# Loading x in column quarters ahead of the weights each multiplies, in a two-layer encoder trunk on one core

## The chip, the cores and the metric

The kernel runs on one core of one Trainium2 chip. The metric is the device time of one execution in microseconds. The engines are named as in the profile: PE is TensorE (PEld its weight loads), ACT is ScalarE, DVE is VectorE, POOL is GpSimd, SP is SyncE; SPq and ACTq are the parts of SP and ACT that issue DMA transfers.

## What is computed

x has 256 rows of 1024 columns. Two layers follow one another; layer 0 mixes tokens with a recurrence (RWKV-7), layer 1 with stick-breaking attention:

```python
def swiglu(x, w_gate, w_up, w_down):
    return (jax.nn.silu(x @ w_gate) * (x @ w_up)) @ w_down

for i in range(DEPTH):
    x = layer_norm(ALPHA * x + 0.5 * swiglu(x, ffn1_w_gate[i], ffn1_w_up[i], ffn1_w_down[i]), ...)
    proj = x @ (rwkv_w_in if i == 0 else sb_w_in)
    heads = concatenate([mix(proj[...]), memory_attention(proj[...], mem_k, mem_v)])
    x = layer_norm(ALPHA * x + heads @ w_out[i], ...)
    x = layer_norm(ALPHA * x + 0.5 * swiglu(x, ffn2_w_gate[i], ffn2_w_up[i], ffn2_w_down[i]), ...)
```

All is float32, and the weights (301 MB read in all) pass through the core once.

## The kernel before, in words

The 256 rows are two halves of 128 (`hf` 0 and 1). Both lie transposed in `xTh` and `xTl`: a float32 value is split into a part that the fast matmul format float32r holds (`hi`, copied out by ACT) and the rest (`lo`, subtracted by DVE). A product of x with weights is three matmuls in one PSUM bank: hi·hi, hi·lo, lo·hi (`mm3`). The 2816 columns of a feed-forward layer are cut into 11 blocks of 256 (`ffn_block`). A block's gate and up weights come as four *pieces* of two k-rows each (`piece`: 256 KB of gate and 256 KB of up into one `raw` buffer, then `hi` by ACT and `lo` by DVE); k runs over the 8 column groups of x. The first block of the program multiplies both halves, with one PSUM bank for each.

No engine's order is that of the code. `Plan` records every operation; `order` then simulates the engines with a cost model (`LAND` is the time it gives a transfer to land) and takes operations by priority; `issue` emits them. The priorities are a table found offline by a search over the same model (`URGENCY`). Operations recorded inside `nc.together()` go out as one. Because everything is emitted at one place, nearly all instructions have line L789 in the profile (L786 in the changed kernel). DMA transfers carry eight completion semaphores in turn, so the ninth is issued only when the first has landed. SP issues nearly all transfers, in order; those of the first piece are issued by ACT.

At the start, nine matmuls on zeros (`warm`) run while data come in. `load_x(hf)` loads one half of x in two transfers of 512 columns (256 KB each) and `turn_x` transposes it in two groups of four on PE (the identity matrix for it is in `cst`), each followed by one ACT copy to `xTh` and one DVE subtraction to `xTl`. Half 0 is loaded before the first block is recorded, half 1 inside it; the plan puts half 1's transfers after all four pieces of the first block:

```python
    load_x(0)
    warm(WARM[1], max(o.i for o in nc.ops if o.eng == "PE"))
```

In the profile of before, the first piece is `raw_9r`, `hi_7r`, `lo_8r`; the next three are 12/10/11, 15/13/14 and 18/16/17 in the same sense. `ps_29r` is the bank of half 0, `ps_30r` that of half 1, `ps_5r` and `ps_6r` are the banks for transposes, `ps_3r` receives the warming matmuls.

Of the kernel before, what the change touches and what calls it, by code (L numbers as in the profile page):

```python
# [129 lines left out]
LAND = 3200.0  # L130
WINDOW = 3413.0
# [12 lines left out]
    '(T`_hY~DVEN35^W4I!+&C&ovw2;nl<9cVu{J+8+e$5`KWUv=*t_B-LL7>nq84K*52IfUm5h49A{A=GjF=juLjK#aSe)PsjZxaG+h=fc8+B|})ChI'
    '^g=n(LR_9^-x1S#e>Et$&Mg<6~-HFoe<eI(fHxFIAg6V>~c0ggdQeaVvOR8sjqSXzF^0_5a-55W0R5WA{lhe%dR9#gE1~y<d!5yTZxUA$(sxgf;f'
    'wd0vcn>rel^F^;_@gq%%6n42RNe#xnh*1Dr}2;Vtx!95{tdmx1WI>$JESO_hqy7w|YX&vLYKg5_#&r^@UuIqd~O~2m=;a#s6hMB&7V;uH-2ysG;Z'
    'y$_tPs0$_=ZkSlwNyB-H^s-s_*#h&vZrG_Qx4W=+tWuO9C|Ls8<YMO3t`vgF~)B~m^$43N5N}M$5Vr0Wpj+ZvSkUSYUBx7&i@nh)Jlam*QDe2i_&'
    'ovEH`k>Y`rO74-fLCLU;G-+23oP_xr`U&xJ6knp%$zVeNnE_)Bg5?H}XcpSzd3%&QZ^mXqmtv}`Ke3*RND$G8h-U+o&>$+q_RPzb$RhcM>l7;{@|'
    'o?7sJV~kI`?%|ng1~bjC3E>#rmbfy68LrU{mb3o>8+q|GhVWrd=c!+9SjvTm<u8gct?uXC>#plV7&R2OX2kfrTD}Fd9qNT}YLjww#OoC?F2U2+-j'
    '4AJxX$Ns^sx}Wm>T0OxOnD7I<CDk6{_mf>ccpu2XE^0@1tV8xKRi<)s68UkKe&yWt^XdJ4>dAP^xi^t6;I+@)&c#+r;hZSTL0e|JH_6xcur<IL#k'  # L150
    'I_v$eoKa>iCFHgsbFf!G3&RWR-TBKt+9C~L}jAyS-g%Llb<43ODp*?=kp2n-_nm#wEhLfG}dwU4=@MFO{A#83A2Q_fF4_%`RrDw(1;U?Vvn05?>*'
    'B@yRuI^s|XY}x#{w*CDW1ZO{e1k7XXkz*ic<CELEqgzFC>=k$&K_w(kvl@T2A)U4=Pvg@i*o}<*z;Am0ekEB!R0sUSaMwm52^K2IR4f5>A0T`tl5'
    'R%*3-Hj?c3;Dbm}$rF9~1W2FLj44863!Rdwv6W-9cckyUnwaBWS!IT6C7-_o(6wVl%Ed*G&k`qttpZ`_QNG;GyYwSK|t>htiF7-!ZEVg5(-;!zrZ'
# [1775 lines left out]
```

## Time and profile before

| | us |
|---|---|
| median of 3 runs | 1057.22 |
| lowest, highest | 1055.42, 1058.07 |
| span of the profiled execution | 1055.1 |
| PE busy | 1039.6 (99% of the span) |
| DVE busy, ACT busy | 885.9 (84%), 740.6 (70%) |

The time of the profiled execution is not listed apart from its span; the span is 0.3 us below the lowest and 2.1 us below the median of the three runs. A span runs from the first to the last instruction. PE's matmuls are pipelined, and a busy share near 100% says that the queue of matmuls is never empty, not that the array is at its peak. Rows of the timeline read: start, duration, engine, line, operation, output<-inputs, shapes, how many merged; in brackets the idle time ahead and what ended it.

### The profile page before, as it was taken

The numbers are of one execution on the slowest core, as the hardware profiler recorded it, in microseconds if no ns is written. First come the engines' busy times: TensorE is split into PE (matmuls) and PEld (weight loads), VectorE is DVE, ScalarE is ACT, GpSimd is POOL, SyncE is SP. The second block draws the span as 40 slices with busy tenths as digits, with TensorE's granted clock in tenths as the row PEclk, the third lists the DMA queues.
The fourth block names the chain that finished last, engine by engine and source line by source line (L and its number), as shares of the span: only waits on it lengthen the run. The fifth ranks groups of instructions, "written<-read, shape, count | busy, mean of one in ns | idle before, by whom it ended". The sixth has DMA issues, their size and how long they took to land.

```text
span 1055.1 us, 17845 instructions
## 1 busy us (share of the span) xinstructions
PE 1039.6 (99%) x6275; PEld 833.2 (79%) x6275; DVE 885.9 (84%) x1241; ACT 740.6 (70%) x1064; POOL 5.3 (0%) x20
## 2 busy tenths in 40 slices
PE   8999999999899999999999999999999999999997
PEld 7888888877688776788888888888778777778885
DVE  6776579999899997898799765569899999976788
ACT  6665568878789877567678454557987998765663
POOL 0000000000000000000000000000000000000000
PEclk9999999999999999999999999999999999999999
DMA  9997869879499788799999966758989989998892
GB/s 314 339 366 252 265 202 352 276 239 328 152 326 332 261 270 281 245 352 324 288 346 346 328 205 217 233 187 286 370 303 322 363 278 322 333 348 266 280 316 80
DMA packets 212684, 303.19 MB, mean 287 GB/s; under 512 B 13892, under 2 KB 159728, under 8 KB 212594
## 3 DMA queue, kind: packets, MB, share of 16 engines
q1 hardware_dynamic: 212050, 301.53, 85.8%
q8 instruction: 49, 0.80, 0.3%
q10 hardware_dynamic: 544, 0.52, 0.2%
q14 instruction: 41, 0.34, 0.1%
HBM read 300.95 MB, written 1.05 MB: 286 GB/s over the span
## 4 chain that ended last, share of the span: by engine, by line
PE 96%; DVE 1%; DMA 1%; SPq 0%; ACT 0%; issue 0%; DVEq 0%; ACTq 0%
PE ps_29r L789 29%; PE ps_30r L789 28%; PE ps_25r L789 8%; PE ps_27r L789 8%; PE ps_26r L789 8%; PE ps_3r L789 8%; PE ps_5r L789 3%; PE ps_6r L789 3%; DMA raw_9r<-in_ffn_w_down_dram 1%; DMA raw_12r<-in_ffn_w_up_dram 0%; DVE x L789 0%; SPq L789 0%; DVE L_345r L789 0%; DVE st_573r L789 0%; DVE idle_2r L789 0%
## 5 line engine op out<-in xcount | busy, mean ns | idle before, releaser
L789 PE MATMUL ps_30r<-lo_11r,xTh 128*128 128x512 f32 x78 | 30.4, 390 | 0.0
L789 PE MATMUL ps_29r<-lo_11r,xTh 128*128 128x512 f32 (+1 forms) x76 | 29.3, 386 | 0.6 <-DVE lo_11r L789 0.6
L789 ACT ACTIVATE idle_2r<-ps_29r 128x256 f32<-128x256 f32 (+1 forms) x35 | 14.8, 424 | 17.1 <-PE ps_29r L789 16.7
L789 ACT ACTIVATE idle_1r<-ps_30r 128x256 f32<-128x256 f32 (+1 forms) x31 | 12.9, 417 | 18.5 <-PE ps_30r L789 18.4
L789 PE MATMUL ps_30r<-hi_13r,xTh 128*128 128x512 f32 x60 | 24.5, 408 | 0.0
L789 PE MATMUL ps_30r<-lo_41r,xTh 128*128 128x512 f32 x62 | 24.2, 390 | 0.0
L789 PE MATMUL ps_30r<-hi_40r,xTh 128*128 128x512 f32 (+1 forms) x60 | 23.8, 396 | 0.0
L789 PE MATMUL ps_30r<-hi_13r,xTl 128*128 128x512 f32 x60 | 23.5, 391 | 0.0
L789 ACT ACTIVATE idle_2r<-ps_30r 128x256 f32<-128x256 f32 (+1 forms) x23 | 9.9, 432 | 19.2 <-PE ps_30r L789 19.2
L789 PE MATMUL ps_30r<-lo_14r,xTh 128*128 128x512 f32 x60 | 23.4, 390 | 0.0
L789 PE MATMUL ps_29r<-hi_13r,xTh 128*128 128x512 f32 (+1 forms) x56 | 23.1, 413 | 0.0
L789 PE MATMUL ps_30r<-hi_40r,xTl 128*128 128x512 f32 (+1 forms) x60 | 23.0, 384 | 0.0
L789 PE MATMUL ps_29r<-lo_17r,xTh 128*128 128x512 f32 (+1 forms) x60 | 23.0, 383 | 0.0
L789 PE MATMUL ps_29r<-hi_10r,xTh 128*128 128x512 f32 x56 | 22.8, 407 | 0.0
L789 PE MATMUL ps_29r<-lo_14r,xTh 128*128 128x512 f32 x58 | 22.6, 390 | 0.0
L789 PE MATMUL ps_29r<-hi_7r,xTh 128*128 128x512 f32 x54 | 22.3, 413 | 0.2 <-ACT xTh L789 0.2
L789 ACT ACT_TABLE_LOAD x16 | 20.5, 1283 | 2.0 <-issue 1.7
L789 PE MATMUL ps_29r<-hi_10r,xTl 128*128 128x512 f32 x56 | 21.9, 392 | 0.0
L789 PE MATMUL ps_29r<-lo_41r,xTh 128*128 128x512 f32 x56 | 21.8, 390 | 0.0
L789 PE MATMUL ps_29r<-hi_49r,xTh 128*128 128x512 f32 x54 | 21.7, 401 | 0.0
L789 PE MATMUL ps_29r<-hi_13r,xTl 128*128 128x512 f32 (+1 forms) x56 | 21.5, 383 | 0.0
L789 PE MATMUL ps_29r<-hi_7r,xTl 128*128 128x512 f32 x54 | 21.2, 393 | 0.2 <-DVE xTl L789 0.2
(2160 smaller groups left out, 3936.6 us busy)
## 6 DMA issues: line engine op xcount, KB each, us to landing
raw_9r<-in_ffn_w_down_dram SPq DMA_DIRECT2D x22, 512.0 KB, 5.8
raw_12r<-in_ffn_w_down_dram SPq DMA_DIRECT2D x19, 512.0 KB, 5.3
raw_48r<-in_ffn_w_gate_dram SPq DMA_DIRECT2D x36, 256.0 KB, 4.8
raw_48r<-in_ffn_w_up_dram SPq DMA_DIRECT2D x36, 256.0 KB, 5.3
raw_18r<-in_ffn_w_gate_dram SPq DMA_DIRECT2D x32, 256.0 KB, 4.6
raw_18r<-in_ffn_w_up_dram SPq DMA_DIRECT2D x32, 256.0 KB, 5.5
raw_51r<-in_ffn_w_gate_dram SPq DMA_DIRECT2D x31, 256.0 KB, 5.0
raw_51r<-in_ffn_w_up_dram SPq DMA_DIRECT2D x31, 256.0 KB, 5.9
```

Source lines behind the costliest of these rows:

```text
L789: fn(*[at(x) for x in a], **{n: at(x) for n, x in k.items()})
```

## The change

- x is loaded as eight transfers of 128 x 256 (128 KB): for each quarter of the columns, one of half 0 and one of half 1. In the code a quarter stands ahead of the piece of weights that it multiplies. Before there were four transfers of 128 x 512.
- The first piece comes in four transfers of 128 KB in place of two of 256 KB: those of its first k-row from ACT, those of its second from SP.
- The transposes of a quarter are recorded just ahead of the products that use it: the first quarter as two groups of two (one for each half), the others as one group of four over both halves, so that one copy and one subtraction serve both. There are 32 transposes in all before and after.
- The products of k below 4 in the first block are recorded singly and no longer three together, so the plan may put other work between them.
- The cost model takes 1700 ns and not 3200 for a transfer to land in the first 6 us, and the table of priorities is a new one. It reorders blocks of matmuls in many places of the program.

```diff
-XPARTS = 2
+LAND0 = 1700.0
+SOON = 6000.0
-URGENCY = ( ... )
+URGENCY = ( ... )
-                landed = max(t + LAND + 400.0 * o.fine, landed) + o.kb * 1024 / 330.0
+                landed = max(t + (LAND if t >= SOON else LAND0) + 400.0 * o.fine, landed) + o.kb * 1024 / 330.0
...
-        made = [(queue or nc.sync).dma_start(v(raw)[..., i * m:(i + 1) * m], src) for i, src in enumerate(srcs)]
+        if queue is None:
+            made = [nc.sync.dma_start(v(raw)[..., i * m:(i + 1) * m], src) for i, src in enumerate(srcs)]
+        else:
+            made = [(nc.sync if k else queue).dma_start(v(raw)[:, k, i * m:(i + 1) * m], src[:, k])
+                    for k in range(shape[0]) for i, src in enumerate(srcs)]
+            for o in made[2:]:
+                nc.in_turn("load", o)
...
-    def mm3(o, sh, sl, wh, wl, start, stop):
+    def mm3(o, sh, sl, wh, wl, start, stop, apart=False):
+        if apart:
+            nc.tensor.matmul(o, sh, wh, start=start, stop=False)
+            nc.tensor.matmul(o, sh, wl, start=False, stop=False)
+            nc.tensor.matmul(o, sl, wh, start=False, stop=stop)
+            return
...
-    def load_x(hf):
-        xs[hf] = xp.tile([P, D], F32, tag=f"x{hf}", name=nm("x"))
-        for n in range(XPARTS):
-            sl = slice(n * D // XPARTS, (n + 1) * D // XPARTS)
+    def load_x(g):
+        sl = slice(2 * g * P, 2 * (g + 1) * P)
+        for hf in range(NHALF):
             nc.in_turn("load", nc.sync.dma_start(xs[hf][:, sl], x[0, half_sl(hf), sl]))
-        turn_x(hf)
+    def turn_part(g):
+        for both in [range(NHALF)] if g else [[hf] for hf in range(NHALF)]:
+            pt = ps("tp")
+            n = len(both)
+            with nc.together():
+                for j in range(2):
+                    for i, hf in enumerate(both):
+                        at = slice((j * n + i) * P, (j * n + i + 1) * P)
+                        nc.tensor.transpose(pt[:, at], xs[hf][:, (2 * g + j) * P:(2 * g + j + 1) * P], ident)
+            sp = pt[:, :2 * n * P].rearrange("p (k t) -> p k t", k=2)
+            hi, lo = (t[:, 2 * g:2 * g + 2, both[0] * P:(both[-1] + 1) * P] for t in xTt)
+            nc.scalar.activation(hi, sp, AF.Copy)
+            nc.vector.tensor_sub(lo, sp, hi.bitcast(F32))
...
+        for k in range(KT):
+            if begin and k % 2 == 0:
+                turn_part(k // 2)
+                if k == 0:
+                    warm(WARM[1], max(o.i for o in nc.ops if o.eng == "PE"))
+            wh, wl = (t[:, k % 2] for t in gu[k // 2])
+            for hf in halves:
+                mm3(o[hf], xT[hf][0][:, k], xT[hf][1][:, k], wh, wl, k == 0, k == KT - 1, begin and k < 4)
...
-    load_x(0)
-    warm(WARM[1], max(o.i for o in nc.ops if o.eng == "PE"))
```

The order that the plan makes of it stands below for the three places that matter. `x_78` is half 0 and `x_79` half 1 in both kernels. In the changed kernel the first piece is `raw_8r`, `hi_6r`, `lo_7r`, the second `raw_11r`, `hi_9r`, `lo_10r`, the third `raw_14r`; `ps_28r` is the bank of half 0, `ps_29r` that of half 1, `ps_30r` and `ps_31r` are the banks for transposes.

The issue of transfers at the start on SP, before:

```order
L789 DMA cst<-in_const_dram 128x128
L789 DMA x_78<-in_x_dram 128x512 x2
L789 DMA raw_12r<-in_ffn_w_gate_dram 128x2x256
L789 DMA raw_12r<-in_ffn_w_up_dram 128x2x256
L789 DMA raw_15r<-in_ffn_w_gate_dram 128x2x256
L789 DMA raw_15r<-in_ffn_w_up_dram 128x2x256
L789 DMA raw_18r<-in_ffn_w_gate_dram 128x2x256
L789 DMA raw_18r<-in_ffn_w_up_dram 128x2x256
L789 DMA x_79<-in_x_dram 128x512 x2
```

and now:

```order
L786 DMA x_79<-in_x_dram 128x256
L786 DMA raw_8r<-in_ffn_w_gate_dram 128x256
L786 DMA raw_8r<-in_ffn_w_up_dram 128x256
L786 DMA cst<-in_const_dram 128x128
L786 DMA raw_11r<-in_ffn_w_gate_dram 128x2x256
L786 DMA raw_11r<-in_ffn_w_up_dram 128x2x256
L786 DMA x_78<-in_x_dram 128x256
L786 DMA x_79<-in_x_dram 128x256
L786 DMA x_78<-in_x_dram 128x256 x3
L786 DMA x_79<-in_x_dram 128x256 x2
L786 DMA raw_14r<-in_ffn_w_gate_dram 128x2x256
```

The identity (`cst`) moved from first to fourth; half 1's first quarter leads, and half 0's first quarter stands behind the second piece.

PE at the start, after nine warming matmuls, before:

```order
L789 MATMUL ps_5r<-cst,x_78 128x128 x4
L789 MATMUL ps_6r<-cst,x_78 128x128 x4
L789 MATMUL ps_3r<-idle_1r 128x128
L789 MATMUL ps_29r<-hi_7r,xTh 128x512
L789 MATMUL ps_29r<-lo_8r,xTh 128x512
L789 MATMUL ps_29r<-hi_7r,xTl 128x512
L789 MATMUL ps_29r<-hi_7r,xTh 128x512
L789 MATMUL ps_29r<-lo_8r,xTh 128x512
L789 MATMUL ps_29r<-hi_7r,xTl 128x512
L789 MATMUL ps_29r<-hi_10r,xTh 128x512
```

and now:

```order
L786 MATMUL ps_31r<-cst,x_79 128x128 x2
L786 MATMUL ps_3r<-idle_1r 128x128
L786 MATMUL ps_29r<-hi_6r,xTh 128x512
L786 MATMUL ps_30r<-cst,x_78 128x128 x2
L786 MATMUL ps_29r<-lo_7r,xTh 128x512
L786 MATMUL ps_29r<-hi_6r,xTl 128x512
L786 MATMUL ps_29r<-hi_6r,xTh 128x512
L786 MATMUL ps_29r<-lo_7r,xTh 128x512
L786 MATMUL ps_29r<-hi_6r,xTl 128x512
L786 MATMUL ps_28r<-hi_6r,xTh 128x512
L786 MATMUL ps_28r<-lo_7r,xTh 128x512
```

Two transposes and a warming matmul now stand ahead of the first product in place of eight and one, and half 0's first two transposes stand between the first product and the second. Behind these rows come eight transposes (second and third quarter), six products, four transposes (last quarter), and from there products alone; before, two groups of four transposes stand after 12 and after 18 products.

ACT at the start, before:

```order
L789 DMA raw_9r<-in_ffn_w_gate_dram 128x2x256
L789 DMA raw_9r<-in_ffn_w_up_dram 128x2x256
L789 ACT_TABLE_LOAD
L789 ACTIVATE idle_2r<-idle_1r 128x1
L789 ACTIVATE hi_7r<-raw_9r 128x512 x2
L789 ACTIVATE xTh<-ps_5r 128x4x128
L789 ACTIVATE xTh<-ps_6r 128x4x128
L789 ACTIVATE hi_10r<-raw_12r 128x1024
```

and now:

```order
L786 DMA raw_8r<-in_ffn_w_gate_dram 128x256
L786 ACT_TABLE_LOAD
L786 ACTIVATE idle_2r<-idle_1r 128x1
L786 DMA raw_8r<-in_ffn_w_up_dram 128x256
L786 ACTIVATE xTh<-ps_31r 128x2x128
L786 ACTIVATE hi_6r<-raw_8r 128x512 x2
L786 ACTIVATE hi_9r<-raw_11r 128x1024
L786 ACTIVATE xTh<-ps_30r 128x2x128
```

ACT's second transfer moved behind the load of the function table, and the first copy of x ahead of the first copy of weights.

More of the change, by code (lines that the diff above doesn't have):

```diff
@@ L144 @@
[L144 to L153, printed above, removed]
@@ new lines @@
+    '|H~di!IB}Y%M?QYUt-LAMF@kp#`saL5Dr!h;p2@lUU_8*e=Z8)mgiy|a9Idldd4_xNC*{A$GGtu?|&8JgjQm{KE}>{#9K6k8Q;e^)Vd9>31MKK5FYu}'
+    '^<#`r77n4>rWh~UUtV$id{YSdj>PzkHCEmjLM8j(?wszgIKFWRW4wP(oS9F?IQ?RbEpms@x>E@6m5Q-On-F&RX)oS;PQ`emHQHAXA=uMfhhp4UFocov'
+    '^>*eEt{ENU)(1m4TOx$R@-eDN2v4WQ?L8?8ZS6npr}2^)$H-Zgt|4@i|0VW+s!|A7Y>4qrd$@4GI`Z7?@fa6>8p7-H`morhPLk{XA-pTTT;IjmaiChr'
+    '!|P*XoTw%{)Z@laVq8^B4b)+pIG=XjZ6CxqQjMov8bV1m&3U<aoHyjB7|V<A(HtQZ$Qi;1Kg&@*HFfS4@>oJlQ>VpP_4W`t{uARawJsvwRbo5gy+!uW'
+    'psHi#dWc#sR@(uaV{Gc0<@U$evuuoS{Sm@#u(nq|hC8=b<q)>J<`b^f=rMU%6T+|m3*q5iF@F6=j8h&8;Xm=bxZCkJhwxm55Uw2NJh8Wzy8^EHyYmOi'
@@ new lines @@
+    '?Zx+E?B5aAR>b&*^%p%ILLvLgwlv0RE7j{z2&3Vs{EQfHn4vCee$u(WI{v-8<W3ADN2;HE-@Z7;`LBntHG7O}*2OsQo)CU39zws;A@mem=5OJux0=H1'
+    '5xsGZe)yzfD(u*sjt5_Y$-dUUJI20)Vfyh9zPXT&cmEJVb!#?-k<mG0TyLF5Fug`C>g%&#U}A>-e4xHH<hRGG;@BF(oHt{v4_hN14Pj$0eO5FTE_naJ'
+    '2V%?(Ge=;rh<p$EI>sL#2;thdVk`>7PwJtAg=4&SPYAnU;<ML6cs8cv&-3Bnuw3U%h2rC~gc+63#~}+Z##hUPaK;)pIq!#VAzWWKgchA+{0gq3<F~=n'
+    'FVDu9MXYUmdcR=^BjB&<#dI9xx;tm#hm9eu*dAlQ8X-K^Q2$KROZuvfbB^o(5^}ucoc!stuUdxiO#c`Q>5rjsaBsC3o5{y8Is5tzI81m+ji-s@OZ_^&'
+    'QjE*x@aY`zojDaM!|ni>Soc|skNq8E%Qi7y0;@yuQWgEbQ9?^pk8zpxPpDnFMtW{}j8|Fj3;o>!?@UmmM%KAkkBqXH9XM}WbJrLTFR*ZRrx?p#mkQ^b'
@@ L1004, in ffn_block @@
         fs = slice(c * FC, (c + 1) * FC)
-        gu = [piece((2, 2 * FC), *(v[:, 2 * g:2 * g + 2, fs] for v in (gv, uv)),
-                    queue=nc.scalar if None in xs and g < 1 else None) for g in range(4)]
+        begin = None in xs
+        if begin:
+            xs[:] = [xp.tile([P, D], F32, tag=f"x{hf}", name=nm("x")) for hf in range(NHALF)]
+        gu = []
+        for g in range(4):
+            if begin:
+                load_x(g)
+            gu.append(piece((2, 2 * FC), *(v[:, 2 * g:2 * g + 2, fs] for v in (gv, uv)),
+                            queue=nc.scalar if begin and g < 1 else None))
         if whole:
@@ L1050, in ffn_block @@
         o = {hf: ps("gu") for hf in halves}
-        apart = [[hf] for hf in halves] if None in xs and not FLAGS["bo"] else [halves]
-        for group in apart:
-            for hf in group:
-                if xs[hf] is None:
-                    load_x(hf)
-            for k in range(KT):
-                wh, wl = (t[:, k % 2] for t in gu[k // 2])
-                for hf in group:
-                    mm3(o[hf], xT[hf][0][:, k], xT[hf][1][:, k], wh, wl, k == 0, k == KT - 1)
-                yield
+        for k in range(KT):
[6 more added lines that the diff above has]
+                mm3(o[hf], xT[hf][0][:, k], xT[hf][1][:, k], wh, wl, k == 0, k == KT - 1, begin and k < 4)
+            yield
         hs = {}
```

282 lines of the change are left out of this document (139 added, 143 removed).

## Prediction

> **What bounds the kernel.** I read the page's engine shares and its chain first, then a table of busy time by stage, then PE's waits, then the timeline of the first 15 us with the issue of transfers.
>
> ```profile
> span 1055.1 us, 17845 instructions
> PE 1039.6 (99%) x6275; PEld 833.2 (79%) x6275; DVE 885.9 (84%) x1241; ACT 740.6 (70%) x1064; POOL 5.3 (0%) x20
> ...
> PE 96%; DVE 1%; DMA 1%; SPq 0%; ACT 0%; issue 0%; DVEq 0%; ACTq 0%
> ```
>
> PE carries 96% of the chain that ended last and stands idle for 1055.1 - 1039.6 = 15.5 us. Where those lie, by stage (the column behind the length is PE busy):
>
> ```profile
> 0.00:12.00 12.00, 8.99 (x45) 6.99 (x45) 4.94 (x6) 6.78 (x9) 1.45 (x10) 1.00 0.89 294
> 12.00:200.00 188.00, 187.97 (x885) 155.12 (x884) 144.87 (x186) 127.49 (x182) 0.21 (x1) 1.00 0.92 301
> 200.00:300.00 100.00, 96.65 (x1145) 74.58 (x1144) 94.94 (x168) 75.77 (x136) 2.40 (x6) 1.00 0.73 244
> ...
> 400.00:500.00 100.00, 98.72 (x896) 75.64 (x896) 86.91 (x119) 66.56 (x87) 0.00 (x0) 1.00 0.90 303
> 500.00:1045.00 545.00, 545.00 (x2591) 441.54 (x2590) 451.07 (x575) 377.47 (x497) 0.00 (x0) 1.00 0.87 290
> 1045.00:1055.10 10.10, 2.21 (x16) 1.89 (x14) 7.01 (x18) 0.20 (x1) 0.00 (x0) 0.83 0.29 105
> ```
>
> 3.0 us of idle lie in the first 12 us, 7.9 us in the last layer norm, 3.4 us between 200 and 300, 1.3 us between 400 and 500; elsewhere PE never stops. The change edits only the first stage, and part of what counts as busy there is warming on zeros. PE's named waits:
>
> ```profile
> PE ps_6r L789 <- DVE L_345r L789: 1.8, 2, 1.2
> ...
> PE ps_6r L789 <- DMA x<-in_x_dram: 0.6, 1, 0.6
> ...
> PE ps_29r L789 <- DVE lo_11r L789: 0.6, 1, 0.6
> ...
> PE ps_5r L789 <- DMA x<-in_x_dram: 0.4, 1, 0.4
> ```
>
> The first belongs to the recurrence and not to the start; the other three are the start. It in order of time:
>
> ```profile
> 0.73 0.38 SPq L789 DMA_DIRECT2D cst<-in_const_dram  x1
> 0.99 3.61 PE L789 MATMUL ps_3r<-idle_1r 128*128 128x128 f32 x18 [0.99 <-POOL lastc L789]
> 1.22 0.49 ACTq L789 DMA_DIRECT2D raw_9r<-in_ffn_w_up_dram  x1
> 1.74 1.28 ACT L789 ACT_TABLE_LOAD   x1 [1.74 <-issue]
> 3.04 0.20 ACT L789 ACTIVATE idle_2r<-idle_1r 128x1 f32<-128x1 f32 x1
> 4.98 0.63 PE L789 MATMUL ps_5r<-cst,x 128*128 128x128 f32 x4 [0.38 <-DMA x<-in_x_dram]
> 5.64 1.15 ACT L789 ACTIVATE hi_7r<-raw_9r 128x512 fp32r<-128x512 f32 x2 [2.40 <-DMA raw_9r<-in_ffn_w_up_dram]
> 6.31 1.29 DVE L789 TENSOR_TENSOR lo_8r<-raw_9r,hi_7r 128x512 fp32r<-128x512 f32 x2 [6.31 <-ACT hi_7r L789]
> 6.70 0.57 ACT L789 ACTIVATE xTh<-ps_5r 128x512 fp32r<-128x512 f32 x1
> 7.33 0.50 PE L789 MATMUL ps_29r<-hi_7r,xTh 128*128 128x512 f32 x1 [0.21 <-ACT xTh L789]
> 7.92 1.06 ACT L789 ACTIVATE hi_10r<-raw_12r 128x1024 fp32r<-128x1024 f32 x1 [0.15 <-DMA raw_12r<-in_ffn_w_up_dram]
> 9.01 1.23 DVE L789 TENSOR_TENSOR lo_11r<-raw_12r,hi_10r 128x1024 fp32r<-128x1024 f32 x1 [0.21 <-ACT hi_10r L789]
> 9.38 1.06 ACT L789 ACTIVATE hi_13r<-raw_15r 128x1024 fp32r<-128x1024 f32 x1 [0.40 <-DMA raw_15r<-in_ffn_w_up_dram]
> 10.92 1.06 ACT L789 ACTIVATE hi_16r<-raw_18r 128x1024 fp32r<-128x1024 f32 x1 [0.49 <-DMA raw_18r<-in_ffn_w_up_dram]
> 11.56 0.66 PE L789 MATMUL ps_5r<-cst,x 128*128 128x128 f32 x4
> 11.97 0.47 PE L789 MATMUL ps_29r<-hi_13r,xTh 128*128 128x512 f32 x1
> 13.79 0.48 PE L789 MATMUL ps_30r<-hi_7r,xTh 128*128 128x512 f32 x1
> 14.11 0.39 PE L789 MATMUL ps_30r<-lo_8r,xTh 128*128 128x512 f32 x1
> 14.34 0.40 PE L789 MATMUL ps_30r<-hi_7r,xTl 128*128 128x512 f32 x1
> ```
>
> Transfers pace the start. With only half 0 of x there, 512 KB of weights feed six products, and a product is 14.34 - 14.11 = 0.23 us: 1.4 us of work for 1.5 us of loading (9.38 to 10.92). When PE starts its 19th product at 13.79, it has done 18 products and 16 transposes; from 11.56 on it no longer waits.
>
> **The change part by part.** I work out when PE has 18 products and 16 transposes behind it now, and compare with 13.79.
>
> *Landing.* Transfers land in the order of the queue: 1600 KB (cst 64, half of x 512, first and second piece) had landed at 7.92, 2112 at 9.38, 2624 at 10.92. That is 2.93 us per 1000 KB, so landing = 7.92 + (KB - 1600) x 0.00293. For the first part of x, behind 576 KB with ACT's share, it gives 4.92; the transposes began at 4.98. In the new order the identity is again at 576 KB: 4.92. The first transposes gain nothing.
>
> *First weights.* ACT's second transfer stands behind the table load. With one issue of 0.49 us less ahead, the load runs from 1.25 to 2.53, the activation ends at 2.75, the issue at 3.25. Among SP's transfers that is place 704 to 960 KB: 5.3 to 6.05. I take 5.7, nearest to the 5.64 at which the same weights came before. Meanwhile two transposes end at 5.4, and a copy of 256 columns (row below: 0.37 us) ends at 5.8. The first half of `hi_6r` runs 5.85 to 6.43 (1.15/2), so the first product starts at 6.5, 0.8 us earlier.
>
> ```profile
> L789 ACT ACTIVATE hT_60r<-ps_5r x4: 363/367/368, 58.4 to 154.4; 128x256 fp32r<-128x256 f32 x4
> L789 DVE TENSOR_TENSOR hT_60r<-ps_5r,hT_60r x4: 417/422/425, 58.8 to 155.2; 128x256 fp32r<-128x256 f32 x4
> ```
>
> *The new wait.* PE then stands at half 0's transposes, whose quarter is at 576 + 128 + 512 + 128 = 1344 KB: 7.17. All products queue behind them; they go on at 7.6 (0.41 us later, as 11.56 to 11.97). Their `lo_7r` needs 6.45 + 0.65 = 7.1 for its first half and 7.75 for its second, so it is hidden. Five products end at 7.6 + 5 x 0.23 = 8.75.
>
> *Second bank.* It needs half 0's copy: `hi_9r` (weights at 1216 KB, 6.8) holds ACT from 7.05 to 8.1, the copy ends at 8.5. Two products end at 9.2.
>
> *Eight transposes.* Their quarters land by 9.05 (1984 KB). The second group of four reuses the bank that DVE still reads: `lo_10r` 8.15 to 9.4, subtraction to 9.82. So they end at 10.25 (0.45 us worse than 2 x 0.41). Six products: 11.6. Last four transposes (2112 KB, 9.42; bank free at 10.5): 12.0. Four products: 12.95.
>
> 18 products and 16 transposes are done at 12.95 in place of 13.79: 0.85 us gained. From there the third piece (2624 KB, 10.92 as before) has its `lo` at 13.3, and PE asks for it at 14.5; no later wait comes.
>
> Transfers: six more on SP. Eight in flight now hold some 1.1 MB and not 2, but at 7.2 us 1280 KB are under way, 3.8 us of the rate above, so the pipe doesn't run dry. SP's issue waits are hidden by that store; ACT has three copies more and DVE three subtractions more but no more columns: about 0.1 us each for starting, beside PE's work.
>
> *The new table.* Between 12 and 200 and from 500 to 1045 us PE is idle for 0.03 us: moving matmuls there can gain nothing, and can lose what a late operand costs, at most one wait like the longest named one, 1.2 us. In the recurrence (the 3.4 and 1.3 us) twelve `S,qr` pairs stand directly ahead of twelve `L,Tt` products before and now, so the 1.2 us wait on `L_345r` stays. From a gain of all 4.7 us to a loss of 1.2 I take 0, by the row that did not move.
>
> *Sum.* 1055.1 - 0.85 = 1054.2 us of span. The median stands 2.1 us above the span, so 1057.2 - 0.85 = 1056.4 us. Less than 0.3% (3.2 us) can't be told from no change here: the three runs alone spread over 2.6 us.
>
> **Rivals.**
>
> *Smaller transfers are slower.* Eight of 128 KB for x, four for the first piece. The early flow was slower than the later:
>
> ```profile
> 2.00:4.00 2.00, 2.00 (x12) 2.00 (x12) 0.00 (x0) 1.23 (x2) 0.12 (x1) 1.00 0.96 293
> ```
>
> If all 1344 KB move at 293 in place of 350 GB/s, half 0's first quarter lands 1344 KB x (3.49 - 2.93) ns = 0.75 us later, all of it on PE's path: gain 0.1 us, 1057.1. Against it: at 11.56 x had landed on the line of the weights, though its rows are twice as long. The Trainium skill, "DMA: Bandwidth & Descriptors", section Bandwidth, says to batch transfers to 1 MiB for most of the peak and has 64 KB at 138 GB/s against 341 for 1 MB; that is for a transfer alone, and this trace with several 256 KB transfers queued keeps 350.
>
> *Slower: PE falls back to its slow phase.* The first 18 passes on zeros took 3.61 us, 0.20 each; the same shape later:
>
> ```profile
> L789 PE MATMUL ps_3r<-idle_1r x20: 274/421/580, 1.0 to 6.8; 128*128 128x128 f32 x20
> ```
>
> 421 in the middle against 274 at best: a factor 1.54 until the start had warmed. Now PE does two transposes, one warming matmul, one product and two transposes from 4.6 to 7.6, about 1.1 us in 3.0, less than before (some 1.5 in 2.7). Should the slow phase come back at 7.6 for as long as it lasted (3.6 us), it costs 3.6 x (1 - 1/1.54) = 1.26 us: 0.4 us slower than before, 1057.6. It decides if so thin a load counts as idle; against it, the granted clock reads 1.00 in every window up to 1045. The Trainium skill, "TensorE: Matmul & The Clock Gate", Part 1, has the clock halved after an idle window of about 3.4 us; by that figure the loss would be an estimated 1.7 us and the sum 1058.1. No trace here shows such a fall after the start.
>
> *The quarter lands early.* If half 0's first quarter comes by 6.6, `lo_7r` at 7.1 is next: gain 1.35 us, 1055.9.
>
> *The table decides.* New filler covers the recurrence's waits: up to -4.7 us more, 1051.7. Or several late operands: three of 1.2 us bring 1060.
>
> **Chances.** The sum as worked out, with the early quarter (gain 0.3 to 1.4): 0.60. Smaller transfers slower (-0.3 to +0.3): 0.18. Slow phase: 0.11. Table better by over 3.2 us: 0.06. Table worse by over 3.2 us: 0.05. Only the last two leave the 0.3% band: faster 0.06, same 0.89, slower 0.05. The range takes the first three, 1055.8 to 1057.6, and the spread of the runs' median around them (half of 2.6 us on either side, widened below for part of the table's gain): 1053.9 to 1058.6.
>
> **What would show it.** The first product at about 6.5; PE waiting there for x until 7.2 and named so; the second bank's first product at 8.75; no PE wait from 12 us to 200; the wait on the recurrence's `L` still 1.2 us. Wrong if half 0's quarter lands after 8, if 128x512 products pitch at more than 0.23 us, or if PE shows idle time beyond 500 us.

## The result: about 2.3 us slower

| | before | after |
|---|---|---|
| median of 10 runs each, us | 1056.96 | 1059.52 |
| lowest, highest | 1055.42, 1060.03 | 1056.74, 1060.45 |
| ratio after / before, 95% interval | | 1.0022 [1.0012, 1.0031] |

The ratio, by the means, makes 2.3 us of it; the medians lie 2.6 us apart. The forecast of 1056.4 us with no measurable change was wrong; the interval excludes 1, and 1059.52 lies above the range. First the page of the changed kernel and its busy time by stage (columns as in the prediction: PE busy stands behind the length; the last three are the granted clock, the busy share of the DMA engines and GB/s):

```profile
span 1057.7 us, 17845 instructions
PE 1041.9 (99%) x6275; PEld 836.0 (79%) x6275; DVE 886.1 (84%) x1242; ACT 740.7 (70%) x1065; POOL 5.3 (0%) x20
```

```profile
0.00:12.00 12.00, 8.87 (x35) 7.36 (x36) 3.28 (x5) 4.21 (x7) 1.45 (x10) 0.87 0.79 240
12.00:200.00 188.00, 187.78 (x879) 154.64 (x879) 144.18 (x183) 127.64 (x181) 0.21 (x1) 1.00 0.91 302
200.00:300.00 100.00, 96.49 (x1146) 74.78 (x1145) 93.72 (x170) 75.36 (x138) 2.41 (x6) 0.98 0.71 240
...
500.00:1045.00 545.00, 545.00 (x2592) 441.91 (x2592) 452.39 (x574) 380.28 (x500) 0.00 (x0) 1.00 0.88 292
```

Idle time is 15.8 us against 15.5, but PE is busy for 2.3 us more with the same 6275 matmuls. Two entries of the clock column are below 1.00 where they were not before, and the flow of the first 12 us fell from 294 to 240 GB/s. PE's waits:

```profile
PE ps_30r L786 <- DVE L_346r L786: 1.8, 2, 1.2
PE ps_31r L786 <- DMA cst<-in_const_dram: 1.1, 1, 1.1
...
PE ps_29r L786 <- ACT hi_6r L786: 0.8, 1, 0.8
```

The recurrence's wait is as before. New is the wait for the identity. The start in order of time, SP's issues first, then ACT's, PE's and ACT's work (a row with x7 runs from the start of the first of seven instructions to the end of the last):

```profile
2.11 0.43 SPq L786 DMA_DIRECT2D cst<-in_const_dram  x1
...
3.06 0.47 SPq L786 DMA_DIRECT2D raw_11r<-in_ffn_w_up_dram  x1
4.00 3.68 SPq L786 DMA_DIRECT2D x<-in_x_dram  x7
8.08 0.38 SPq L786 DMA_DIRECT2D raw_14r<-in_ffn_w_gate_dram  x1
...
1.23 0.39 ACTq L786 DMA_DIRECT2D raw_8r<-in_ffn_w_up_dram  x1
...
6.31 0.41 PE L786 MATMUL ps_31r<-cst,x 128*128 128x128 f32 x2 [1.11 <-DMA cst<-in_const_dram]
...
7.71 0.51 PE L786 MATMUL ps_29r<-hi_6r,xTh 128*128 128x512 f32 x1 [0.77 <-ACT hi_6r L786]
8.48 0.44 PE L786 MATMUL ps_30r<-cst,x 128*128 128x128 f32 x2 [0.27 <-DMA x<-in_x_dram]
...
9.86 0.63 PE L786 MATMUL ps_29r<-lo_7r,xTh 128*128 128x512 f32 x1
10.29 0.63 PE L786 MATMUL ps_29r<-hi_6r,xTl 128*128 128x512 f32 x1
...
15.68 0.40 PE L786 MATMUL ps_29r<-hi_9r,xTh 128*128 128x512 f32 x1
...
20.16 1.06 ACT L786 ACTIVATE hi_41r<-raw_43r 128x1024 fp32r<-128x1024 f32 x1 [1.68 <-DMA raw_43r<-in_ffn_w_up_dram]
22.87 0.44 PE L786 MATMUL ps_30r<-cst,idle_2r 128*128 128x128 f32 x2 [0.22 <-DVE idle_2r L786]
```

Three things are seen. SP takes 3.68 us for seven transfers of 128 KB (249 GB/s where 350 flowed before), and its next weights go out at 8.08. One issue of these takes 0.33 to 0.43 us, 2.72 us for the seven; for the rest SP stands until an earlier transfer has landed, 1.7 us in four waits between 3.53 and 8.08. Products at 9.86 and 10.29 are 0.43 us apart and not 0.23: the clock is at half. And the 19th product starts at 15.68, not 13.79. The first fall lasts from about 9.0 to 12.4 us. The second is in the recurrence, shown by a row of busy time over 3 us:

```profile
279.00:282.00 3.00, 2.35 (x82) 2.19 (x75) 1.80 (x5) 2.00 (x5) 0.00 (x0) 0.50 0.10 22
```

Four theories went into the experiments: *issue* (many small transfers make the bytes late), *clock gate* (thin load lets the clock fall), *late data* (identity and half 0's quarter come late in the queue) and *table* (the new priorities cost time elsewhere).

### The profile page after: what moved, and what is told of

The parts are those of the page before. It is cut to its first block, busy times and chain, and to the rows that moved or that the text cites. A ratio compares the mean times of both kernels' runs of the same rounds, so it can differ in the third digit from the quotient of the medians.

```text
span 1057.7 us, 17845 instructions
## 1 busy us (share of the span) xinstructions
PE 1041.9 (99%) x6275; PEld 836.0 (79%) x6275; DVE 886.1 (84%) x1242; ACT 740.7 (70%) x1065; POOL 5.3 (0%) x20
## 4 chain that ended last, share of the span: by engine, by line
PE 96%; DMA 2%; DVE 1%; ACT 0%; issue 0%; SPq 0%; DVEq 0%
PE ps_29r L786 30%; PE ps_28r L786 26%; PE ps_3r L786 9%; PE ps_24r L786 8%; PE ps_26r L786 8%; PE ps_25r L786 8%; PE ps_31r L786 3%; PE ps_30r L786 3%; DMA raw_43r<-in_ffn_w_up_dram 1%; DMA raw_11r<-in_ffn_w_up_dram 0%; DMA raw_14r<-in_ffn_w_up_dram 0%; DVE x L786 0%; DVE L_346r L786 0%; SPq L786 0%; ACT Y_341r L786 0%
## 5 line engine op out<-in xcount | busy, mean ns | idle before, releaser
L786 PE MATMUL ps_29r<-lo_7r,xTh 128*128 128x512 f32 x84 | 33.1, 394 | 0.0
L786 PE MATMUL ps_29r<-lo_10r,xTh 128*128 128x512 f32 x74 | 29.1, 393 | 0.0
L786 PE MATMUL ps_29r<-hi_41r,xTh 128*128 128x512 f32 (+1 forms) x64 | 26.5, 413 | 0.0
L786 PE MATMUL ps_28r<-lo_10r,xTh 128*128 128x512 f32 x66 | 25.7, 390 | 0.0
L786 PE MATMUL ps_29r<-lo_42r,xTh 128*128 128x512 f32 x64 | 24.9, 390 | 0.0
L786 PE MATMUL ps_29r<-hi_41r,xTl 128*128 128x512 f32 (+1 forms) x64 | 24.6, 384 | 0.0
L786 PE MATMUL ps_28r<-hi_6r,xTh 128*128 128x512 f32 x58 | 24.2, 418 | 0.0
L786 PE MATMUL ps_29r<-hi_12r,xTh 128*128 128x512 f32 x58 | 23.6, 407 | 0.0
L786 PE MATMUL ps_29r<-hi_50r,xTh 128*128 128x512 f32 x58 | 23.1, 399 | 0.0
L786 PE MATMUL ps_28r<-hi_6r,xTl 128*128 128x512 f32 x58 | 22.8, 393 | 0.0
```

The costliest lines, as they stand in the source:

```text
L786: fn(*[at(x) for x in a], **{n: at(x) for n, x in k.items()})
```

## Experiments

Eighteen kernels, 5 to 12 timed runs each, compared with runs of the kernel before on the same chip. The clock is the mean over a kernel's runs (155 runs of the kernel before: 0.9961; the ten of the changed kernel: 0.9950).

| kernel | base and edit | median us | ratio to before [95%] | clock |
|---|---|---|---|---|
| before_again | before, unchanged | 1057.65 | 1.0003 [0.9993, 1.0012] | 0.9951 |
| start_only | changed start, old order behind | 1062.00 | 1.0044 [1.0032, 1.0057] | 0.9948 |
| table_only | old start, new order behind | 1060.85 | 1.0034 [1.0022, 1.0046] | 0.9970 |
| warm | after, 24 warming matmuls more | 1065.19 | 1.0070 [1.0057, 1.0083] | 0.9946 |
| warm_wide | after, two warming matmuls four times as wide | 1059.46 | 1.0017 [1.0008, 1.0026] | 0.9960 |
| cst_first | after, identity first | 1059.24 | 1.0021 [1.0011, 1.0031] | 0.9955 |
| x_early | after, identity and both first quarters first | 1060.17 | 1.0027 [1.0017, 1.0038] | 0.9956 |
| x_early_warm | x_early and warm_wide | 1059.33 | 1.0018 [1.0009, 1.0026] | 0.9963 |
| xw_late | x_early_warm, recurrence's loads later | 1059.92 | 1.0015 [1.0006, 1.0024] | 0.9961 |
| x_on_act | after, seven transfers of x from ACT | 1060.25 | 1.0023 [1.0015, 1.0032] | 0.9948 |
| thick | after, old sizes | 1057.83 | 1.0003 [0.9993, 1.0013] | 0.9968 |
| before_thin | before, new sizes | 1059.43 | 1.0019 [1.0008, 1.0030] | 0.9951 |
| before_slots | before, as many transfers, cut by rows | 1060.31 | 1.0027 [1.0016, 1.0039] | 0.9948 |
| x_thick | after, x alone in old sizes | 1060.10 | 1.0023 [1.0014, 1.0032] | 0.9954 |
| thick_late | thick, recurrence's loads later | 1057.68 | 1.0002 [0.9993, 1.0011] | 0.9966 |
| before_fill | before, three more matmuls in the recurrence | 1056.43 | 0.9990 [0.9981, 0.9999] | 0.9978 |
| after_fill | after, the same three | 1058.61 | 1.0015 [1.0006, 1.0024] | 0.9971 |
| thick_late_fill | thick_late, the same three | 1057.14 | 0.9998 [0.9989, 1.0007] | 0.9977 |

### How much is chance: before_again

> The kernel before, unchanged, as its own control. It gives the granted clock of each of its runs, which only one profile gave so far, and says how far two sets of runs of one kernel differ. Theory 'clock gate' (the changed kernel loses its time where PE's clock falls to half for 3.4 us, at 8.9 to 12.3 us and at 278.7 to 282.0 us): mean clock 0.998 in most runs, one fall (the tail, after the work) and no fall in the body; ratio 1.000 within 0.001. Rival 'chance' (falls come in the kernel before as often, and the one profile of it happened to have none): clocks of 0.992 to 0.997 in most runs, as in the ten runs of the changed kernel.

The rival came true. This profile of the kernel before has a span of 1058.6 us and a fall of its own, three times as long:

```profile
274.00:279.00 5.00, 4.16 (x113) 3.69 (x116) 2.37 (x7) 3.63 (x12) 0.67 (x3) 0.59 0.01 3
279.00:282.00 3.00, 2.35 (x28) 1.91 (x23) 2.54 (x8) 1.52 (x3) 0.00 (x0) 0.50 0.38 102
282.00:290.00 8.00, 8.00 (x44) 6.70 (x44) 6.74 (x17) 4.36 (x6) 0.00 (x0) 0.80 0.04 13
```

Over the 155 runs of the kernel before the mean clock goes from 0.993 to 0.999, and each 0.001 less comes with 0.68 us more (correlation -0.72). The profile that the forecast was read from had no fall in its body at all. So two single profiles can't simply be subtracted, and the fall in the recurrence is not the change's doing alone.

### The two halves of the change: start_only, table_only

Both replace the table of priorities by an order written out: one half's operations in the one kernel's order, the other 4709 in the other's.

```diff
-            for o, p in zip(self.ops, np.cumsum(step)):
-                o.pri = float(p)
...
+        given = [v >> 1 for v in coded]
+        best = self.order(given)
```

> The changed start (loads by quarters, first weights in four transfers, single products, PE, ACT, DVE and SP in the changed kernel's order for the first block's loads, transposes and products), and for all the rest, 4709 operations, the order of the kernel before on each engine. Theory 'start' (the loss is made in the first 16 us: 19th product 1.9 us late, most of it by the clock at half from 8.9 to 12.3): +1.9 us against before, about 1058.9, clock 0.50 again between 9 and 12, and the wait pattern at 270 to 290 as in before. Theory 'table' (the new table of priorities makes the loss, the start none): 1057.0, no change. Theory 'data' (late identity and late quarter, whatever the clock): +1.9 us too, with or without a fall.

> The start of the kernel before (four transfers of x, identity first) and for the 4709 operations behind the first block's products the changed kernel's order on each engine. Theory 'start': the table costs at most what is left of the 2.6 us, +0.0 to +0.7 us, 1057.0 to 1057.7; if the thinner work at 274 to 279 us makes the clock fall whatever came before, a fall at about 276 to 280 and +0.7. Theory 'table': +2.6 us, 1059.6.

Each was slower than both its parents. Between 12 and 200 us the parents wait for 0.03 and 0.22 us in all; start_only's row of busy time there reads

```profile
12.00:200.00 188.00, 186.22 (x866) 152.13 (x867) 141.96 (x175) 124.55 (x177) 0.20 (x1) 1.00 0.90 299
```

and table_only has 185.12 us of 188. The 1.8 and 2.9 us are all lost before 40 us, near the seam, where an order meets data that come at other times than it was made for. Both are inconclusive on theory *table*.

### Keeping PE busy, and earlier data: warm, warm_wide, cst_first, x_early, x_early_warm

```diff
+        for i, n in ((11, 5), (52, 4), (56, 3)):
+            self.ops[i].calls = self.ops[i].calls + self.ops[52].calls * n
```

> The changed kernel with twelve more matmuls on zeros: five behind the nine at the start, four behind the one after the first transposes, three behind the first product, where PE stood idle for 1.1, 0.8 and 0.3 us. No data come earlier. Theory 'clock gate': PE is busy from 1 us on, the clock stays at 1.00 from 8.8 to 12.4, the product pitch is 0.23 and not 0.43 us, and 1.7 us of the loss go: 1057.8, -1.7 us against the changed kernel's 1059.5. Theory 'data': the first product still waits for the weights and the quarter of half 0 still lands at 8.4: 1059.5, no change, or +0.3 where an extra matmul stands ahead of a product. If the phase of the gate is a matter of chance, the fall may come later in the start.

The last group came out as fifteen matmuls and not three, since the list that it repeats had just been made longer. They held half 0's transposes back to 12.10 us; behind them products pitched at 0.23 us with the clock at 1.00. The 48 passes more also brought waits that nothing in the profile explains, in the recurrence:

```profile
PE ps_30r L788 <- issue: 2.4, 1, 2.4
...
PE ps_31r L788 <- issue: 1.3, 1, 1.3
```

So warm_wide widens two matmuls (operations 11 and 52, `[list(z.ap[0]), [0, 4], [1, P]]` as the moving operand) and adds none. The other three sort SP's transfers:

```diff
+        first = [0, 13, 12]        # cst_first: [0]
+        order = sorted(order, key=lambda x: first.index(x[2].i) if x[2].i in first else len(first))
```

> The changed kernel with as many instructions on PE as before, but the ninth warming matmul and the one behind the first transposes run over 512 columns of zeros in place of 128, so that PE is busy in the gaps at 5.2 to 6.3 and 6.9 to 7.7 us. No data come earlier. Theory 'clock gate in the start' (the thin load from 5.2 to 8.5 us makes the clock fall): clock 1.00 from 7 to 14 us, 0.23 us between products, 19th product at 8.48 + 5.55 = 14.0 us (the stretch from half 0's transposes to the 19th product as the earlier run with warming showed it) in place of 15.7; in time 1.7 us less than the changed kernel, 1057.8, if the fall comes in every run of it, about 0.6 us less, 1058.9, if in one of three. Theory 'data': 1059.5, no change. Theory 'table': 1059.0 or more, as the start is not where the loss is.

> The changed kernel with the identity as the first transfer on SP, and all others one place later. Theory 'late identity' (the first transposes at 6.3 us and not 5.0 cost 1.1 us): first transposes at about 5.2, first product at about 6.7, and 0.7 to 1.1 us less than the changed kernel, 1058.4 to 1058.8. Theory 'late quarter' (all products but one queue behind half 0's transposes, whose quarter is SP's seventh transfer and lands at 8.4): transposes of half 0 still at 8.0 to 8.5, 19th product unchanged, 1059.5. If the identity's 512-byte rows make the dip of the flow at 4.4 to 5.2 us (101 to 133 GB/s), the dip moves to the front and half 0's quarter lands some 0.4 us earlier.

> The changed kernel with SP's first three transfers in the order identity, first quarter of half 1, first quarter of half 0, and then the rest as it was: half 0's quarter is third in place of seventh, ahead of 768 KB of weights. Theory 'late quarter': transposes of half 0 right behind those of half 1, at 5.6 to 6.0 us, products run on from 6.9, 19th product at 12.8 to 13.5 us in place of 15.7, PE busy enough that the clock doesn't fall in the start: 2 to 2.8 us less than the changed kernel, 1056.7 to 1057.5, as fast as the kernel before or 0.5 us faster. Theory 'weights' (the second half of the first weights and the second piece, now later, are the next wait): 19th product at 14.0 to 14.5, gain 1.2 to 1.7 us only if the clock stays up. Theory 'table': 1059 or more.

> Both edits at once: identity and both first quarters first, and the two warming matmuls four times as wide. Theory 'clock gate': against x_early alone a gain only if x_early still shows a fall in the start; else 0 to +0.3 us, as the wide matmul stands ahead of half 0's transposes and of the first product. Theory 'data': the same as x_early. Best case 1056.5, against 1057.6 of the kernel before.

The starts came near to what was expected and the times didn't move by more than their intervals. With the clock kept up or the data early, the 19th product comes at 14.0 to 14.3 us, nearly as early as in the kernel before (13.8 to 14.1); cst_first starts its transposes at 4.99 but still waits for half 0's quarter (8.27). Then all meet one wait. Profiled values, us (before_thin and thick are described in the next section):

| kernel | 19th product | wait for `idle_2r` at 22 us | first `S,qr` product |
|---|---|---|---|
| before | 13.79 | none | 271.27 |
| before_again | 14.05 | none | 271.28 |
| after | 15.68 | 0.22 | 273.33 |
| cst_first | 15.44 | 0.6 | 273.26 |
| x_early | 13.95 | 0.8 | 272.10 |
| warm_wide | 14.24 | 1.35 | 272.76 |
| x_early_warm | 14.29 | 1.46 | 273.15 |
| thick | 14.21 | none | 271.20 |
| before_thin | 15.48 | none | 273.59 |

The last column says how far PE has come ahead of the recurrence; two profiles of the kernel before agree there to 0.01 us. Most of what the start gains is given back at 22 us. x_early keeps 1.2 us of it in its profile and is still no faster over its runs; that profile's clock falls for longer in the recurrence than the changed kernel's. The rows of warm_wide show what is waited for:

```profile
19.85 1.06 ACT L790 ACTIVATE hi_41r<-raw_43r 128x1024 fp32r<-128x1024 f32 x1 [1.44 <-DMA raw_43r<-in_ffn_w_up_dram]
22.56 0.44 PE L790 MATMUL ps_30r<-cst,idle_2r 128*128 128x128 f32 x2 [1.35 <-DVE idle_2r L790]
```

`raw_43r` lands at 19.85 (after: 20.16). ACT and DVE work in order, and the gate's output (`idle_2r` is the buffer of `h`) stands behind `hi_41r` and `lo_42r` there. By the forecast's own line the 4672 KB up to it would have landed at 7.92 + 3072 x 0.00293 = 16.9 us. The flow of the next 8 us, in the kernel before:

```profile
12.00:20.00 8.00, 8.00 (x40) 6.62 (x39) 6.85 (x8) 5.70 (x8) 0.00 (x0) 1.00 1.10 348
```

and in the changed one:

```profile
12.00:20.00 8.00, 8.00 (x41) 6.61 (x41) 6.59 (x7) 5.57 (x7) 0.00 (x0) 0.98 1.06 302
```

With the first 12 us that makes (294 - 240) x 12 + (348 - 302) x 8 = 1.02 MB less by 20 us, 2.9 us of flow. Not all of it is the doing of the sizes: the new table also has the recurrence's loads in these 8 us. Theories *clock gate in the start* and *late data* fall as sufficient causes: with either repaired, the wait for late weights takes the place of the loss.

### Sizes: thick, before_thin, x_on_act, xw_late

thick joins transfers (`wide` sets the column count of an access pattern to 512) and sends identity and both first halves first; before_thin splits them; x_on_act sends operations 12, 23, 34, 28, 22, 29, 35 by ACT; xw_late moves the recurrence's three loads.

```diff
+        for i, gone in ((13, 23), (12, 22), (28, 34), (29, 35)):              # thick
+            self.ops[i].calls, self.ops[gone].calls = [(fn, tuple(wide(x, 1, 512) for x in a), k)], []
...
+        for i in (12, 13, 45, 46):                                             # before_thin
+            self.ops[i].calls = [(fn, tuple(part(x, 1, j) for x in a), k) for j in range(2)]
...
+        moved = [x for x in order if x[2].i in (666, 667, 668)]                # xw_late
```

> The changed kernel with the sizes of transfers of the kernel before: four transfers of x of 128 x 512 (each first quarter with the second, each third with the fourth), two for the first piece, from ACT; identity first, then both first halves of x. PE's, ACT's and DVE's orders are the changed kernel's. Theory 'issue' (SP needs 0.4 to 0.5 us for a transfer of whatever size, so 128 KB each give at most 270 to 340 GB/s where 350 flow; the changed kernel had moved 0.65 MB less than the one before by 12 us and some 1 MB less by 20): flow of 0 to 12 us back from 240 to about 290 GB/s, the piece that the wait at 22 us hangs on (raw_43) lands at 17.5 to 18.5 in place of 20.1, no wait on idle_2r, 1.2 to 2 us less than the changed kernel, 1057.5 to 1058.3. Theory 'rows' (the three loads of the recurrence's weights with 64 rows, which the new table moved from 18 to 13.6 us, take the flow): raw_43 still at 19.5 to 20 and 1059. Theory 'clock gate': depends on the fall in the start alone.

> The changed kernel with the seven later transfers of x issued by ACT and not by SP; sizes and rows are unchanged. Theory 'issue': SP goes on to the next weights at about 4 us and not at 8.08, the flow of 8 to 10 us rises from 256 to about 340 GB/s, raw_43 lands 1 to 2 us earlier, time 0.5 to 1.5 us less than the changed kernel. Rival 'small transfers are slower in themselves': flow and landing unchanged, 1059.5. Rival 'eight in flight': SP and ACT both stand until earlier transfers have landed, and nothing moves.

> The kernel before with the changed kernel's sizes: each of the four transfers of x in two of 128 x 256, the second k-row of the first piece as two transfers of its own on SP, behind half 0 of x. Orders of PE, ACT and DVE as before, so no other part of the change is in it. Theory 'issue': six more transfers, 2.8 us more of SP, of which 1.8 us ahead of the second piece: 19th product 1 to 2 us later than 13.8 to 14.1, flow of 0 to 12 us at 250 to 265 in place of 294 GB/s, time +1 to +2 us, 1058.6 to 1059.6. Theory 'rows' and theory 'table': no change from the kernel before, 1057.6, as the order beyond is its own.

> The changed kernel with identity and both first quarters first, the two wide warming matmuls, and the three loads of the recurrence's weights (384 KB over 64 rows) six transfers later on SP, about where the kernel before has them. Theory 'rows': the flow of 17.5 to 21.5 us rises from 190 to 350 GB/s, raw_43 lands at about 18.5, the wait on idle_2r (1.5 us with the start repaired) goes, 1.4 us less than without the move, 1058.0. Theory 'issue': raw_43 lands at 19 or later, the wait keeps most of its length, 1059. In both the clock can still fall in the recurrence.

thick and before_thin show from both sides that the sizes of the first transfers carry the loss. The changed kernel with the old sizes (and the identity first) is as fast as the one before; the kernel before with the new sizes loses 0.19%, of the change's 0.22%. The first 12 us of thick by busy time, clock and flow:

```profile
0.00:12.00 12.00, 9.21 (x43) 7.69 (x44) 3.84 (x6) 5.22 (x9) 1.45 (x10) 1.00 0.87 287
```

and of before_thin:

```profile
0.00:12.00 12.00, 9.38 (x36) 7.31 (x37) 3.81 (x5) 5.54 (x8) 1.45 (x10) 0.86 0.79 242
```

In before_thin the clock falls in the start and the 19th product comes at 15.48:

```profile
15.48 0.48 PE L797 MATMUL ps_30r<-hi_7r,xTh 128*128 128x512 f32 x1
```

In thick the weights that warm_wide waited for are there 1.7 us earlier, and the profile lists no wait of PE between 14 and 262 us:

```profile
18.19 1.06 ACT L796 ACTIVATE hi_41r<-raw_43r 128x1024 fp32r<-128x1024 f32 x1 [1.27 <-DMA raw_43r<-in_ffn_w_up_dram]
```

thick moves 298 GB/s from 12 to 20 us, no more than the changed kernel, and loses nothing by it: of the 1.02 MB only (287 - 240) x 12 - (302 - 298) x 8 = 0.53 MB comes back with the old sizes, 1.5 us of flow. The rest belongs to the recurrence's loads. x_on_act was a bad test: flow rose to 261 GB/s, but ACT stood in its issues and the first product waited 2.1 us for `hi_6r`. xw_late fell short of 1058.0: the move mended the dip, but with small transfers in front the bytes are late anyway, and PE waited 0.3 us for `idle_2r` at 21 us, 0.8 us for it again at 30 us and 0.3 us for `hT_61r` at 33 us. Theory *rows* (the recurrence's loads over 64 rows are what makes the weights late) falls as a main cause.

### Transfers or bytes: before_slots, x_thick, thick_late

```diff
+            most, last = [(fn, tuple(rows(x, r, n) for x in a), k) for r, n in ((0, 112), (112, 16))]   # before_slots
```

> The kernel before with as many transfers on SP as before_thin, in the same places, but cut by rows: of each of the four transfers of x and the two of the first piece 112 rows go as one transfer and 16 rows as another (the 16 rows of the first piece on SP, behind half 0 of x). Nearly all bytes still come in large transfers, with rows as long as before. Theory 'issue' (each transfer costs SP 0.4 to 0.5 us, whatever its size): six more, the same loss as before_thin, 1059.4 (+2.0), 19th product at about 15.5, flow of 0 to 12 us at 240 to 250 GB/s. Rival 'small transfers or rows of 1 KB flow slower in themselves': 1057.6, 19th product at 14, flow about 285.

> The changed kernel with its own order on SP, identity fourth, and the first piece in four transfers as it has it, but x in four transfers of 128 x 512 and not eight of 128 x 256: four transfers fewer on SP out of the six that the change added. Theory 'issue': two thirds of the loss go, 1058.1 (0.7 us over the kernel before), flow of 0 to 12 us at about 270 GB/s. Rival 'the first piece's four transfers and the late identity carry it': 1059.4.

> The changed kernel with the old sizes (as 'thick') and the three loads of the recurrence's weights six transfers later on SP. Theory 'rows': the dip of the flow at 16 to 20 us (210 and 283 GB/s in 'thick') moves to 22 to 26; as 'thick' showed no wait of PE between 16 and 262 us, nothing is gained, 1057.8. If something in the start still hung on it, up to 0.5 us less, 1057.3. It is slower only if the move makes a wait later.

before_slots moves nearly all bytes in large transfers with long rows and still loses (233 GB/s in the first 12 us): the loss doesn't need halved transfers or rows of 1 KB. It lost more than was expected (19th product at 17.62, not 15.5), and its transfers of 16 rows may flow badly for a reason of their own, which was not tried apart. x_thick refuted my two thirds: four transfers fewer, and nothing gained. Its SP rows give a part of the reason:

```profile
3.06 0.47 SPq L790 DMA_DIRECT2D raw_11r<-in_ffn_w_up_dram  x1
4.73 1.29 SPq L790 DMA_DIRECT2D x<-in_x_dram  x3
```

SP has issued the eighth transfer at 3.53 and stands until one of the first has landed, 1.2 us, with only 1344 KB issued. What the first eight hold orders the kernels in two groups: 1856 KB in before and thick (294 and 287 GB/s over 12 us), 960 to 1344 KB in before_thin, before_slots, x_early, after and x_thick (233 to 248). The time to issue and the limit of eight both count transfers, and in the changed kernel both are seen (2.72 us of issues, 1.7 us of standing); these runs don't part them.

Nor is it only a matter of bytes issued too late. By 7.52 us x_thick had issued 2880 KB (2.95 MB) and moved about 1.6 MB, so some 1.3 MB was under way. Yet it went on like this:

```profile
7.50:10.00 2.50, 2.35 (x6) 1.66 (x7) 2.24 (x4) 1.92 (x4) 0.00 (x0) 1.00 0.86 246
```

The kernel before, with some 1.4 MB under way at 8 us:

```profile
8.00:10.00 2.00, 1.49 (x6) 0.86 (x5) 1.79 (x3) 1.60 (x2) 0.00 (x0) 1.00 1.09 357
```

So a start in small transfers may also flow slower in itself; this rival stays open beside the other two. thick_late is as thick: nothing hung on it.

### The falls in the recurrence: before_fill, after_fill, thick_late_fill

```diff
+        for i, n in ((1163, 512), (1275, 384), (1283, 256)):
+            self.ops[i].calls = [(self.real.tensor.matmul, (out, ident_, moving), dict(start=True, stop=True))] + calls
```

> The kernel before with three more matmuls on PE in the recurrence, identity times constants into a bank that is free there: 512 columns ahead of the products on L (wait 1.2 us), 384 ahead of the transposes behind them (0.8), 256 ahead of the next transposes (0.6). Their outcome is never used. Theory 'clock gate' (the clock falls to half when PE had too little to do in the stretch before, and whether it falls at 272 to 287 us is a matter of the gate's phase): mean clock of the runs up from 0.996 to 0.998, no 0.50 between 272 and 290 us in the profile, the spread of the runs smaller, and 0.7 to 1.5 us less, about 1056.4. Rival 'idle time is not what it measures' (small 64 x 64 products count too little): clock and time unchanged, 1057.6, or +0.3 where an added matmul outlasts its wait.

> The changed kernel with the same three added matmuls in the recurrence. Theory 'issue in the start' (the small first transfers cost 2 us, whatever the clock does later): no 0.50 between 274 and 290 us, 1 us less than the changed kernel, 1058.4, so still 2.0 us over before_fill. Theory 'clock gate in the recurrence' (the changed kernel is slower because its new order there makes the clock fall more often): all of it goes, 1056.4 like before_fill. The fall in the start can still come (0.50 at 8 to 12 us).

> The changed kernel with the old sizes, the recurrence's loads later and the three added matmuls: all three repairs. Theory 'issue': as fast as before_fill, 1056.4 within 0.7; the order by quarters itself is worth nothing here, as bytes pace the start and not the place of x among them. If the new order of the rest is worth the 0.6 us that the profiles seemed to show behind the recurrence, 1055.8, faster than both kernels by 1.8 and 3.6 us.

Three matmuls whose outcome is never used, in waits of 1.2, 0.8 and 0.6 us, make the kernel before faster by 0.10% (the interval just leaves out 1), as expected, and its spread smaller (1055.83 to 1057.22 in 11 runs; 1055.62 to 1059.27 in the 35 beside them). The added matmuls in before_fill's timeline:

```profile
272.16 1.13 PE L795 MATMUL ps_30r<-cst 128*128 128x512 f32 x2
...
274.75 0.91 PE L795 MATMUL ps_30r<-cst 128*128 128x384 f32 x2
...
278.10 0.70 PE L795 MATMUL ps_30r<-cst 128*128 128x256 f32 x2
```

and the stretch by busy time, with the clock at 1.00:

```profile
272.00:290.00 18.00, 17.70 (x214) 13.43 (x207) 15.93 (x37) 13.89 (x28) 0.67 (x3) 1.00 0.18 56
```

after_fill is 2.2 us slower than before_fill by the medians (1058.61, 1056.43), which ran on two chips; measured each against the kernel before on its own chip, it is 0.25%, 2.6 us. Neither profile has a fall in the recurrence, and the loss of the start is still there. after_fill's profile is of the slowest of its eleven runs:

```profile
13.52 0.40 PE L792 MATMUL ps_29r<-hi_9r,xTh 128*128 128x512 f32 x1
...
23.48 0.69 PE L792 MATMUL ps_30r<-cst,idle_2r 128*128 128x128 f32 x2 [2.91 <-DVE idle_2r L792]
```

The 19th product comes 0.27 us earlier than in the kernel before, and PE then stands for 2.91 us. This wait brings a fall of the clock with it, from 23.0 to 26.4 us, so the profile shows more than the wait alone:

```profile
22.50:25.00 2.50, 1.52 (x5) 1.33 (x6) 1.21 (x3) 1.33 (x2) 0.00 (x0) 0.59 0.99 329
25.00:27.50 2.50, 2.50 (x10) 2.01 (x9) 2.41 (x3) 2.05 (x2) 0.00 (x0) 0.72 1.06 367
```

thick_late_fill did not beat before_fill; whether order by quarters and new table are worth anything with the old sizes can't be told. before_fill is the only kernel here whose interval lies below 1.

## Why the prediction was wrong, step by step

- *What bounds the kernel.* That transfers pace the start was right. That PE never stops and its clock is 1.00 up to 1045 held for that one execution.
- *Landing by KB.* Here it failed first. The line came from transfers of 256 KB. Identity 6.31 in place of 4.92, half 0's transposes at 8.48 behind a quarter forecast for 7.17; the order of the queue was read rightly. So one of the prediction's own signs of being wrong came (the quarter after 8 us), and with the pitch of 0.43 us a second.
- *First weights.* ACT's second transfer was issued from 1.23 to 1.62, beside the table load, not from 2.75 to 3.25. It didn't help: `hi_6r` stands on ACT behind the first copy, and that behind the identity. First product 7.71, forecast 6.5.
- *"So the pipe doesn't run dry."* This is the step that decided. The 1280 KB that I counted as under way at 7.2 us had not all been issued, as I left out SP's time: by 8.08 SP and ACT had issued 2112 KB, which the kernel before had issued by 4.52. By 8 us about 1.7 MB of it had moved, so only some 0.4 MB was under way. The six more transfers, which I put at nothing, were not a cost to hide under stored bytes: 1.02 MB is missing by 20 us, 0.53 MB of it by the sizes.
- *"No later wait comes."* Failed with it. Without a fall of the clock the 19th product does come at 13.5 to 14.3 (forecast 12.95), and the wait for `idle_2r` takes it back. I stopped the sum at 13 us, where PE was no longer waiting, though the bytes were.
- *Rival "smaller transfers are slower".* Right in kind, at a chance of 0.18, and sized at 0.75 us on one quarter; followed to 20 us it is 0.53 MB, `raw_43r` 2.0 us later than in thick (20.16, 18.19), and 2 us of time. I set it aside because 256 KB transfers kept 350 GB/s; the first 12 us of thick (287) and before_thin (242) show how much less flows at half the size. The Trainium skill's rule on batching ("DMA: Bandwidth & Descriptors", section Bandwidth) agrees with these two in kind, though before_slots loses as much with most bytes in large transfers.
- *Rival "slow phase".* It came, about as long as assumed (3.4 us, 3.6 assumed) but deeper: 0.43 us a product for 0.23 is a factor of 1.87 and not 1.54, which makes 1.6 us and not 1.26. "No trace here shows such a fall after the start" was a misreading: the clock reads 0.83 in the prediction's own last row, 1045 to 1055.1. But it doesn't decide: warm_wide has no fall in its start and is no faster, since PE was early for its data then.
- *Eight transposes.* From the prediction's own figures they end 0.23 us later than 2 x 0.41 would (9.2 + 0.82, 10.25), not 0.45; the sum goes by 10.25 and isn't touched.
- *The table at nothing.* Not refuted: thick carries it and stands at 1.0003. The hybrids left it open.

## What to carry to other kernels

Count transfers, not only bytes: where the first microseconds are paced by data, splitting transfers for an earlier first product can starve a product many microseconds later. Follow a late flow to the next place where an in-order engine takes its data, and don't end the sum where PE stops waiting. Before subtracting two profiles, look how far the granted clock of repeated runs differs, and fill the waits around which it falls.
